# Hybrid decoder trunk on one core: norms applied behind the products, and the modulation vectors spread over VectorE, ScalarE and GpSimd

## The chip, the core and the metric

One core of a Trainium2 chip runs the whole kernel. A core has TensorE (PE, with its weight loads as PEld), VectorE (DVE), ScalarE (ACT), GpSimd (POOL) and SyncE (SP), whose queue issues almost all transfers here. The metric is the device time of one execution in microseconds. The profile gives the span from the first to the last instruction; the time of an execution also holds what lies around the span.

## The reference, cut to what matters

Two layers work on 256 tokens of width 1024. Each layer norms x, scales and shifts it by vectors that come from the conditioning c, multiplies it by a wide matrix, runs three mixers, projects back and adds; then it does the same with an MLP of width 4096. A last norm ends it.

```
for l in range(DEPTH):                                   # 2 layers
    mod = silu_c @ w_ada[l] + b_ada[l]                   # 6 vectors of 1024
    sh1, sc1, g1, sh2, sc2, g2 = jnp.split(mod[:, None, :], 6, axis=-1)
    h = rmsnorm(x, norm1_g[l]) * (1.0 + sc1) + sh1
    proj = h @ w_in[l]
    u, dq, dk, dv, mq, mk, mv = jnp.split(proj, splits, axis=-1)
    ...                                                  # S5, differential attention, MoBA
    x = x + g1 * (mix @ w_out[l])
    h = rmsnorm(x, norm2_g[l]) * (1.0 + sc2) + sh2
    x = x + g2 * (jnp.square(jax.nn.relu(h @ mlp_w1[l])) @ mlp_w2[l])
return rmsnorm(x, final_g)
```

The rsqrt of the norm is one number per token. The shift is one number per channel. With h = x*ag*r + sh, the product is W^T h = r * (W^T (x*ag)) + W^T sh.

## The kernel before

**Layout.** x is kept transposed: channels on the 128 partitions, 256 tokens in the free dimension, eight tiles `xT[0]` to `xT[7]` in one buffer `xall`. Every weight matrix is cut into units of 128x1024 f32 (512 KB). SyncE's queue loads them in program order into a ring `raw` of three. ScalarE rounds a unit to its high half and VectorE subtracts it for the low half, both in `whl`, a ring of four (`unit`, L111 to L125). A product of a unit with a tile `hx` of two halves is three matmuls (`mm3`): high by high, high by low, low by high.

**A norm between products.** After the back projection (`back_unit`, `back_add`) or the last W2 product, `x_ssq` or `square_in` gather squares, `x_norm` (L418) sums them over the channels with matmuls by ones and makes the rsqrt on ScalarE with one Newton step on VectorE. `norm_h` (L453) then calls `h_tile` (L442) eight times: VectorE multiplies x by the gain and the rsqrt into `hz` (L444), ScalarE adds the shift for the high half of `hx` (L449), VectorE takes the low half (L450). Only then can the next product start. This happens in layer 0 ahead of the MLP, in layer 1 ahead of the first product and ahead of the MLP. Layer 0's first norm is written apart and goes tile by tile with the first loads.

**The MLP.** It runs in two halves. A half is eight W1 steps (`mlp1_mm`, two units and 48 matmuls of 256 columns each, both results in one PSUM bank; `mlp1_act` takes relu, square and the two halves) and eight W2 tiles (`mlp2`, two units each). The hidden tiles stay in SBUF.

**The modulation.** Each of the twelve vectors takes eight tiles of 512 KB. The first two of layer 0 are made at the start. Of the rest, five (ADA_DVE) are summed on VectorE, one multiply-add of 128x1024 per tile (L301); two are done by TensorE in steps among the mixer's work; three (ADA_VEC) are loaded ahead as a whole (`ada_load`) and multiplied by TensorE in one go (`ada_vec`, L258) after the norm's sums and before the normed products, one at each of the three norms.

**Order.** Every engine runs its instructions in the order of the program. That order is set by a scheduler which follows priorities; `issue_after` and the letters of MIXER set parts of it by hand. TensorE's `wk` tiles are four PSUM banks, its `acc` tiles another four.

Of the kernel before, what the change touches and what calls it, by code (L numbers as in the profile page):

```python
# [14 lines left out]
OP = mybir.AluOpType  # L15
# [34 lines left out]
UW = 1024  # L50
N_IN, N_OUT, N_W1 = 20, 8, 32
# [4 lines left out]
def hybrid_trunk(ctx, tc, xT_d, pos_d, par_d, sb_d, sbt_d, scw_d, glu_d, wm_d, wa_d, out_d):  # L56
# [55 lines left out]
    def unit(gate=0):  # L112

        w = raw_unit()
        hl = ring.tile([128, 2, UW], F32R, name="whl", bufs=4)
        hi, lo = hl[:, 0, :], hl[:, 1, :]
        if gate:
            with tc.issue_after(gate_a[0].ins):
                V.tensor_copy(hi, w)
            with tc.issue_after((gate_a if gate == 1 else gate_b)[0].ins):  # L120
                V.tensor_tensor(lo, w, hi.bitcast(F32), op=OP.subtract)
        else:
            A.activation(hi, w, AF.Copy)  # L123
            V.tensor_tensor(lo, w, hi.bitcast(F32), op=OP.subtract)  # L124
        return hl  # L125

    last_mm, last_dve, last_act, gate_a, gate_b, gate_t = [None], [None], [None], [None], [None], [None]
# [132 lines left out]

    def ada_load(l, i):

        u = 16 + ADA.index((l, i)) * 8
        ws = []
        for k in range(3):
            w = ring.tile([128, UW], F32, name="ada", bufs=3)
            nc.sync.dma_start(w, wa_d[u + k])
            ws.append([w])
        half = [(n, c) for n, c in (("vv", 2), ("qk", 2), ("sp_gc", 3), ("at_o", 2)) for _ in range(c)]
        half.append(("sp_pb", 1))  # L270
        for k in range(3, 8):
            ws.append([])
            for h in range(2):
                n, c = half.pop(0)
                w = work.tile([128, UW // 2], F32, name=n, bufs=c)
# [1069 lines left out]
```

## Time and profile before

| what | us |
|---|---|
| median of 3 runs (685.09 to 688.39) | 686.48 |
| the profiled execution | 688.0 |
| its span | 686.3 |
| TensorE busy in the span | 664.8 |
| VectorE busy | 510.1 |
| ScalarE busy | 382.8 |
| GpSimd busy | 21.3 |
| mean granted clock of TensorE, share of full speed | 0.993 |

A page of the profile shows one execution. Busy times of an engine are those of its instructions in the records; matmuls are pipelined and their ends are modelled, so a record of 284 ns may stand 120 ns behind the one before it. The chain of waits follows the work that ended last back through what released it. A view by stretches gives the busy time of each engine between two moments.

### The profile page before, as it was taken

What the parts mean: (1) busy time and instruction counts of PE and PEld (TensorE: products, weight loads), DVE (VectorE), ACT (ScalarE), POOL (GpSimd) and SP (SyncE); (2) the same over time, 40 slices, a digit from 0 to 9 for tenths busy, and PEclk for the clock granted to TensorE, in tenths of its full rate; (3) what the DMA queues carried; (4) which work ended last, traced back from release to release, by engine and by line L of the source; (5) the groups of instructions that cost most, each with busy time, mean ns of one, the idle gap of its engine ahead of it and who ended that gap; (6) DMA issues with size and microseconds to landing.
All of it is one profiled execution on the core that took longest, in us unless ns stands there. A gap on an engine that the chain in (4) does not pass through costs nothing. (4 is left out here: it accounts for less than half of the span.)

```text
span 686.3 us, 13334 instructions
## 1 busy us (share of the span) xinstructions
PE 664.8 (97%) x5182; PEld 583.3 (85%) x5182; DVE 510.1 (74%) x1150; ACT 382.8 (56%) x726; POOL 21.3 (3%) x24
## 2 busy tenths in 40 slices
PE   8899999999999999999999999999999999999994
PEld 6686677988899888999887878799899988999884
DVE  7888979986997897879657788886865555555553
ACT  3566744663566833776443556575476533566540
POOL 0000000000000000000210000000000000000221
PEclk9999999999999999999999999999999999999998
DMA  9987776863989688889855532554256555555531
GB/s 323 408 318 241 247 260 241 295 205 113 315 308 334 231 312 264 308 290 338 299 180 192 187 123 89 168 171 158 94 175 194 185 185 188 179 186 184 189 118 61
DMA packets 45134, 151.96 MB, mean 221 GB/s; under 512 B 5136, under 2 KB 5264, under 8 KB 45072
## 3 DMA queue, kind: packets, MB, share of 16 engines
q1 hardware_dynamic: 44640, 150.60, 63.9%
q8 instruction: 40, 0.66, 0.4%
q10 hardware_dynamic: 432, 0.53, 0.2%
q14 instruction: 22, 0.18, 0.1%
HBM read 150.06 MB, written 1.05 MB: 220 GB/s over the span
## 5 line engine op out<-in xcount | busy, mean ns | idle before, releaser
L124 DVE TENSOR_TENSOR whl<-raw,whl 128x1024 fp32r<-128x1024 f32 x178 | 217.1, 1223 | 106.9 <-ACT whl L123 104.4
L123 ACT ACTIVATE whl<-raw 128x1024 fp32r<-128x1024 f32 x178 | 187.9, 1057 | 143.5 <-PE acc L1016 52.5
L132 PE MATMUL wk<-hx,whl 128*128 128x256 f32 x1536 | 188.2, 284 | 1.2 <-DVE hx L450 1.2
L132 PEld LDWEIGHTS wk<-hx,whl 128*128 128x128 f32 x1536 | 185.3, 191 | 4.2 <-DVE hx L450 2.4
L1022 PE MATMUL acc<-mx,whl 128*128 128x512 f32 x240 | 60.7, 395 | 0.0
L132 PE MATMUL acc<-mx,whl 128*128 128x256 f32 x384 | 51.6, 288 | 0.0
L1022 PEld LDWEIGHTS acc<-mx,whl 128*128 128x128 f32 x240 | 43.0, 188 | 8.7 <-issue 0.8
L132 PEld LDWEIGHTS acc<-mx,whl 128*128 128x128 f32 x384 | 47.5, 191 | 3.0 <-issue 2.3
L301 DVE SCALAR_TENSOR_TENSOR adaacc<-ada,cs,adaacc 128x1024 f32<-128x1024 f32 x35 | 44.8, 1280 | 5.8 <-DMA ada<-in_wa_dram 5.7
L1025 DVE SCALAR_TENSOR_TENSOR xall<-acc,mod,xall 128x256 f32<-128x256 f32 x62 | 29.9, 483 | 20.9 <-PE acc L1016 20.2
L132 PE MATMUL acc<-whl,hx 128*128 128x256 f32 x288 | 40.0, 288 | 0.0
L132 PEld LDWEIGHTS acc<-whl,hx 128*128 128x128 f32 x288 | 36.6, 190 | 3.3 <-issue 1.8
L803 PE MATMUL acc<-whl,hx 128*128 128x512 f32 x96 | 38.5, 404 | 0.0
L805 PE MATMUL acc<-whl,hx 128*128 128x512 f32 x96 | 38.4, 400 | 0.0
L804 PE MATMUL acc<-whl,hx 128*128 128x512 f32 x96 | 38.4, 400 | 0.0
L992 ACT ACTIVATE sp_pa<-wk 128x512 f32<-128x512 f32 x32 | 18.9, 592 | 32.7 <-PE wk L132 31.4
L1016 PEld LDWEIGHTS acc<-mx,whl 128*128 128x128 f32 x256 | 34.8, 190 | 2.5
L1016 PE MATMUL acc<-mx,whl 128*128 128x256 f32 x256 | 35.7, 282 | 0.0
L1022 PE MATMUL acc<-at_e,whl 128*128 128x512 f32 x120 | 33.0, 398 | 0.0
L882 ACT ACTIVATE at_e<-at_e,at_m 128x128 f32<-128x128 f32 (+1 forms) x48 | 21.2, 443 | 8.4 <-DVE at_m L877 8.4
L449 ACT ACTIVATE hx<-hz,mod 128x256 fp32r<-128x256 f32 x32 | 14.9, 502 | 19.2 <-DVE hz L444 19.2
L1022 PEld LDWEIGHTS acc<-at_e,whl 128*128 128x128 f32 x120 | 20.7, 191 | 2.7
(381 smaller groups left out, 1005.4 us busy)
## 6 DMA issues: line engine op xcount, KB each, us to landing
raw<-in_wm_dram SPq DMA_DIRECT2D x184, 512.0 KB, 4.0
ada<-in_wa_dram SPq DMA_DIRECT2D x74, 512.0 KB, 5.9
sp_gc<-in_wa_dram SPq DMA_DIRECT2D x9, 256.0 KB, 4.5
qT<-in_wa_dram SPq DMA_DIRECT2D x4, 512.0 KB, 8.9
adaacc<-in_wa_dram SPq DMA_DIRECT2D x3, 512.0 KB, 9.8
qk<-in_wa_dram SPq DMA_DIRECT2D x6, 256.0 KB, 4.9
vv<-in_wa_dram SPq DMA_DIRECT2D x6, 256.0 KB, 4.1
at_o<-in_wa_dram SPq DMA_DIRECT2D x6, 256.0 KB, 4.2
```

The lines of the kernel that those rows point to most:

```text
L123: A.activation(hi, w, AF.Copy)
L124: V.tensor_tensor(lo, w, hi.bitcast(F32), op=OP.subtract)
L132: last_mm[0] = T.matmul(out, a[:, p, :], b[:, q, :], start=start and i == 0, stop=stop and i == 2, skip_group_check=True)
L301: V.scalar_tensor_tensor(acc, w, cs[:, k + j:k + j + 1], acc, op0=OP.mult, op1=OP.add)
L803: T.matmul(o, h[:, 0, sl], w[:, 0, :], start=(k == 0), stop=False, skip_group_check=True)
L804: T.matmul(o, h[:, 0, sl], w[:, 1, :], start=False, stop=False, skip_group_check=True)
L805: last_mm[0] = T.matmul(o, h[:, 1, sl], w[:, 0, :], start=False, stop=last, skip_group_check=True)
L882: A.activation(e[:, c, ks], e[:, c, ks], AF.Exp, scale=SCALE, bias=mx[:, i:i + 1], accum_out=st[:, i:i + 1])
L992: A.activation(r, ps, AF.Relu)
L1016: last_mm[0] = T.matmul(acc[:, :S], w[:, 1, sl], a[:, 0, :], start=False, stop=last, skip_group_check=True)
L1022: T.matmul(acc, w[:, 0, sl], a.rearrange("p c t -> p (c t)"), start=first, stop=False, skip_group_check=True)
L1025: V.scalar_tensor_tensor(xT[f], acc[:, c * S:(c + 1) * S], mvec(l, 5, f), xT[f], op0=OP.mult, op1=OP.add)
```

## The change

Three things are changed together.

First, the tiles that go into three products (layer 1's first product, and W1 in both layers) are x times the gain, not normed (`p_tile`). Each half of such a tile has two columns more, 258 in place of 256, which hold the shift; GpSimd writes them. The product then carries W^T sh in its last columns. On the way out of PSUM, VectorE multiplies the result by `rb`, which holds the rsqrt in 256 columns and ones in the last two (`p_norm`), and ScalarE adds the product's own shift column as a bias, in the relu or in the copy. The two results of a W1 step now take a PSUM bank each. `x_norm` is called inside the first such product, after its second or third k. In layer 1, after the first product (u), the tiles are made once more, normed, for the other products of the mixer.

Second, the gates that put weight units of a norm behind it go (`unit`), and so do the vectors done in one go (`ada_load`, `ada_vec`). VectorE now sums (0,2), (1,0), (1,1), (1,2) and (1,5); for (0,5), (1,3) and (1,4) ScalarE multiplies a tile by its number and GpSimd adds it. Their ends are eight one-column matmuls. `crep` goes, since `cs` is broadcast where it is read.

Third, the steps are placed anew: G in MIXER, GP_STEPS and V_STEPS in the MLP, each issued with a priority that is later by LATE. The ring `ada` has four tiles in place of three, and some buffers are renamed.

```diff
-        if gate:
-            with tc.issue_after(gate_a[0].ins):
-                V.tensor_copy(hi, w)
-            with tc.issue_after((gate_a if gate == 1 else gate_b)[0].ins):
-                V.tensor_tensor(lo, w, hi.bitcast(F32), op=OP.subtract)
...
+    def ada_one(l, i, k, gp):
+        w = ada_tile(l, i, k)
+        if k == 0:
+            ada_st[l, i] = work.tile([128, UW], F32, name="qT", bufs=3) if gp else big.tile([128, UW], F32, name="adaacc")
+        acc, c = ada_st[l, i], cs[:, k:k + 1]
+        if gp:
+            A.activation(w if k else acc, w, AF.Copy, scale=c)
+            if k:
+                GP.tensor_tensor(acc, acc, w, op=OP.add)
+        elif k == 0:
+            V.tensor_scalar(acc, w, c, None, op0=OP.mult)
+        else:
+            V.scalar_tensor_tensor(acc, w, c, acc, op0=OP.mult, op1=OP.add)
+        if k == 7:
+            def fin():
+                cp = wk_tile()
+                for f in range(KT):
+                    T.matmul(cp[:, f:f + 1], acc[:, f * 128:(f + 1) * 128], ones[:, 0:1], start=True, stop=True)
...
+    def p_tile(l, k, ag, i_sh):
+        h = h_buf(k)
+        sh = mvec(l, i_sh, k).to_broadcast([128, SX - S])
+        GP.tensor_copy(h[:, 0, S:], sh)
+        GP.tensor_tensor(h[:, 1, S:], sh, h[:, 0, S:].bitcast(F32), op=OP.subtract)
+        hi, lo = h[:, 0, :S], h[:, 1, :S]
+        A.activation(hi, xT[k], AF.Copy, scale=ag)
+        V.scalar_tensor_tensor(lo, xT[k], ag, hi.bitcast(F32), op0=OP.mult, op1=OP.subtract)
+        return h
+
+    def p_norm(ps):
+        t = work.tile([128, 2, SX], F32, name="sp_pa", bufs=2)
+        for i in range(2):
+            V.tensor_tensor(t[:, i], ps[i][:, :SX], rb, op=OP.mult)
+        return t
...
-            h = norm_h(l, "n1", 0, 1, x_rest(), vec)
-            uT = Chunk("u", h).run().u_out()
-            cm = Chunk("qk", h).run(1)
+            cu = Chunk("p", pts).run(lambda: x_norm(*x_rest()))
+            h = [h_tile(l, k, ag[:, k:k + 1], 0, rb[:, :S]) for k in range(KT)]
+            cm = Chunk("qk", h).run()
+            uT = cu.u_out()
...
-        vec = ada_load(l, 5)
         back_unit(accs, mixed[4:6], False, True)
-        back_add(accs, l, 2)
-        h = norm_h(l, "n2", 3, 4, x_ssq(), vec)
+        ag = norm_gain(l, "n2", 4)
+        pts = []
+        for f in range(KT):
+            back_add(accs, l, 2, f)
+            pts.append(p_tile(l, f, ag[:, f:f + 1], 3))
+        sq = x_ssq()
...
+    GP_STEPS = (1, 1, 1, 1, 2, 2, 2, 2, 1, 1, 1, 1, 2, 2, 0, 0)
+    V_STEPS = (1, 2, 2, 2, 2, 2, 2, 2, 2, 2, 2, 2, 1, 0, 0, 0)
```

How it stands in the engines' order, at three places.

TensorE at layer 1's second norm, before, from the last matmul of the back projection (`mx` are the mixers' results, L387 and L432 the norm's sums, L258 the vector of the modulation done in one go):

```order
L132 MATMUL acc_5684<-mx5_4466,whl_5901 128x256 x3
L387 MATMUL wk_5959<-qT_5957,ones_78 32x256 x4
L387 MATMUL wk_5959<-qT_5958,ones_78 32x256 x2
L432 MATMUL wk_5976<-qT_5958,ones_78 128x256 x2
L432 MATMUL wk_5976<-sq_5972,sel_80 128x256
L258 MATMUL wk_5988<-ada_5865,crep_96 32x256 x4
```

The same place after (L365 and L423 are now the norm's sums, `hx0` the first tile of x by its gain, L127 the product):

```order
L127 MATMUL acc_5747<-mx5_4563,whl_5932 128x256 x3
L365 MATMUL wk_6032<-qT_6030,ones_78 32x256 x4
L127 MATMUL wk_6047<-hx0_5983,whl_6051 128x258 x3
...
L127 MATMUL wk_6047<-hx3_6001,whl_6051 128x258 x2
L365 MATMUL wk_6032<-qT_6031,ones_78 32x256 x2
L127 MATMUL wk_6047<-hx3_6001,whl_6051 128x258
L127 MATMUL wk_6048<-hx3_6001,whl_6056 128x258
L423 MATMUL wk_6077<-qT_6031,ones_78 128x256 x2
L127 MATMUL wk_6048<-hx3_6001,whl_6056 128x258 x2
L127 MATMUL wk_6047<-hx4_6007,whl_6051 128x258
L423 MATMUL wk_6077<-sq_6045,sel_80 128x256
```

The norm's sums moved from ahead of the products into the first step's middle, and the vector of the modulation is gone from there.

TensorE at layer 1's first product, after (L1035 is the last W2 product; L423 the norm's sums; L811 the second product, with the tiles made anew):

```order
L1035 MATMUL acc_4493<-vv_4027,whl_4525 128x256
L127 MATMUL acc_4566<-hx0_4091,whl_4570 128x258 x3
L127 MATMUL acc_4567<-hx0_4091,whl_4570 128x258 x3
L127 MATMUL acc_4566<-hx1_4144,whl_4570 128x258 x3
L127 MATMUL acc_4567<-hx1_4144,whl_4570 128x258 x3
L423 MATMUL wk_4586<-sg_t_4087,ones_78 128x256
L423 MATMUL wk_4586<-sq_4585,ones_78 128x256
L127 MATMUL acc_4566<-hx2_4258,whl_4570 128x258 x3
...
L127 MATMUL acc_4567<-hx7_4553,whl_4610 128x258 x3
L811 MATMUL acc_4673<-whl_4677,hx0_4639 128x512
```

Before, the first product stood behind the norm, and its matmuls alternated with those of the second; now it stands ahead of and around the norm's sums, and the second follows it.

VectorE around layer 0's first W2 half, after (L119 is the low half of a weight unit, L281 and L279 a modulation step, L1044 the addition to x):

```order
L1044 SCALAR_TENSOR_TENSOR xall_74<-acc_2973,mod0_101,xall_74 128x256
L279 TENSOR_SCALAR adaacc_3031<-ada_3029,cs_95 128x1024
L604 SCALAR_TENSOR_TENSOR sg_z_3271<-sg_z_3271,tb_c_2581 128x256
L281 SCALAR_TENSOR_TENSOR adaacc_3031<-ada_3151,cs_95,adaacc_3031 128x1024
L119 TENSOR_TENSOR whl_3122<-raw_3120,whl_3122 128x1024
L119 TENSOR_TENSOR whl_3170<-raw_3168,whl_3170 128x1024
```

GpSimd there, after (the sum of a modulation vector):

```order
L277 TENSOR_TENSOR qT_3020<-qT_3020,ada_3022 128x1024
L277 TENSOR_TENSOR qT_3020<-qT_3020,ada_3143 128x1024
L277 TENSOR_TENSOR qT_3020<-qT_3020,ada_3147 128x1024
L277 TENSOR_TENSOR qT_3020<-qT_3020,ada_3257 128x1024
L277 TENSOR_TENSOR qT_3020<-qT_3020,ada_3261 128x1024
```

GpSimd before, from its set-up on (`sqs` is the sum of squares in the second W2 half):

```order
L96 AFFINE_SELECT mask_82<-mask_82 128x128
L99 IOTA tau_87 128x128
L1039 TENSOR_SCALAR sqs_4022<-sq_4020 128x256
L1041 TENSOR_TENSOR sqs_4022<-sqs_4022,sq_4069 128x256
L1041 TENSOR_TENSOR sqs_4022<-sqs_4022,sq_4163 128x256
```

Before, GpSimd had nothing to do between the set-up and the second W2 half; now it has seven additions in the first W2 half, beside VectorE's own steps.

## Rows read from the trace of the kernel before

The columns stand in the first line of each group. Numbers in brackets at a row's end are idle time ahead of it and what ended it.

**Rows 1.** The first part of the page: busy us, share of the span, instructions.

```profile
PE 664.8 (97%) x5182; PEld 583.3 (85%) x5182; DVE 510.1 (74%) x1150; ACT 382.8 (56%) x726; POOL 21.3 (3%) x24
```

**Rows 2.** Groups of instructions: busy us, mean ns of one, idle time before them.

```profile
L124 DVE TENSOR_TENSOR whl<-raw,whl 128x1024 fp32r<-128x1024 f32 x178 | 217.1, 1223 | 106.9 <-ACT whl L123 104.4
...
L123 ACT ACTIVATE whl<-raw 128x1024 fp32r<-128x1024 f32 x178 | 187.9, 1057 | 143.5 <-PE acc L1016 52.5 <-DMA raw<-in_wm_dram 45.5 <-PE acc L132 13.6
...
L301 DVE SCALAR_TENSOR_TENSOR adaacc<-ada,cs,adaacc 128x1024 f32<-128x1024 f32 x35 | 44.8, 1280 | 5.8 <-DMA ada<-in_wa_dram 5.7
...
L700 DVE TENSOR_TENSOR sp_pa<-wk,tb_c 128x256 f32<-128x256 f32 x16 | 6.7, 416 | 0.8 <-PE wk L696 0.8
...
L444 DVE SCALAR_TENSOR_TENSOR hz<-xall,ag,sp_s 128x256 f32<-128x256 f32 x32 | 14.4, 480 | 0.2
```

**Rows 3.** The chain of waits in order of time: start us, us, what.

```profile
489.50 3.59 PE wk L258 x64
493.09 23.80 PE wk L132 x192
...
517.24 23.13 PE wk L132 x192
540.36 1.84 PE acc L1022 x8
```

**Rows 4.** Busy time of each engine in four stretches of layer 0's MLP.

```profile
core 0: us, PE busy (x) PEld busy (x) DVE busy (x) ACT busy (x) POOL busy (x), PEclk, DMA share, GB/s
173.10:222.30 49.20, 48.02 (x392) 46.94 (x389) 43.23 (x69) 30.77 (x51) 0.00 (x0) 1.00 0.92 319
222.30:269.30 47.00, 47.00 (x280) 40.33 (x279) 39.17 (x60) 26.41 (x45) 0.00 (x0) 1.00 0.77 272
269.30:316.70 47.40, 47.40 (x400) 46.85 (x400) 40.04 (x50) 33.58 (x54) 0.00 (x0) 1.00 0.85 301
316.70:364.20 47.50, 47.50 (x348) 41.92 (x348) 29.71 (x36) 22.20 (x31) 9.44 (x7) 1.00 0.74 253
```

**Rows 5.** Timeline, layer 1's second norm: start us, us, engine, line.

```profile
483.06 0.87 DVE L970 SCALAR_TENSOR_TENSOR xall<-acc,mod,xall 128x256 f32<-128x256 f32 x2
...
486.96 0.88 DVE L970 SCALAR_TENSOR_TENSOR xall<-acc,mod,xall 128x256 f32<-128x256 f32 x2 [0.56 <-PE acc L132]
...
493.02 7.15 PE L132 MATMUL wk<-hx,whl 128*128 128x256 f32 x53
```

**Rows 6.** Timeline of TensorE, layer 1's first norm.

```profile
363.95 0.28 PE L1016 MATMUL acc<-qT,whl 128*128 128x256 f32 x1
...
370.02 0.39 PE L132 MATMUL acc<-hx,whl 128*128 128x256 f32 x1 [0.39 <-ACT hx L449]
...
387.57 0.39 PE L803 MATMUL acc<-whl,hx 128*128 128x512 f32 x1
```

**Rows 7.** Timeline of GpSimd, and of VectorE, at the end of layer 1.

```profile
643.63 1.23 DVE L124 TENSOR_TENSOR whl<-raw,whl 128x1024 fp32r<-128x1024 f32 x1
...
644.14 1.31 POOL L1041 TENSOR_TENSOR sqs<-sqs,sq 128x256 f32<-128x256 f32 x1 [4.18 <-ACT sq L1036]
...
672.23 0.74 POOL L1041 TENSOR_TENSOR sqs<-sqs,sq 128x256 f32<-128x256 f32 x1 [4.31 <-ACT sq L1036]
680.09 1.67 POOL L1232 TENSOR_TENSOR sp_s<-sp_pa,sp_s 128x512 f32<-128x512 f32 x1 [7.12 <-DVE sp_s L439]
```

**Rows 8.** The last multiplies, by their line: duration ns min/median/max, starts.

```profile
L1232 DVE TENSOR_TENSOR qT<-qk,sp_s x2: 692/1220/1748, 680.0 to 680.6; 128x512 f32<-128x512 f32 x2
```

**Rows 9.** Timeline, layer 0's second norm: a weight unit, and TensorE.

```profile
158.31 1.23 DVE L124 TENSOR_TENSOR whl<-raw,whl 128x1024 fp32r<-128x1024 f32 x1 [2.00 <-ACT whl L123]
...
166.92 1.06 PE L387 MATMUL wk<-qT,ones 128*32 128x256 f32 x12
...
182.42 4.82 PE L132 MATMUL wk<-hx,whl 128*128 128x256 f32 x38 [0.35 <-DVE hx L450]
```

More of the change, by code (lines that the diff above doesn't have):

```diff
@@ L228, in ada_finish @@
     def ada_finish(l, i, row):
-        rs = work.tile([128, 256], F32, name="adarow", bufs=1)
+        rs = work.tile([128, 256], F32, name="sg_t", bufs=2)
         A.activation(rs, row, AF.Copy)
@@ L257, in ada_mm @@
             c = (g % per) * 256
-            T.matmul(row[32 * g:32 * g + 32, :], crep[:, k, :], w[g // per][:, c:c + 256],
+            T.matmul(row[32 * g:32 * g + 32, :], cs[:, k:k + 1].to_broadcast([128, 32]), w[g // per][:, c:c + 256],
                      start=(k == 0), stop=(k == 7), tile_position=(0, 32 * g), skip_group_check=True)
[L261 to L275, printed above, removed]
-                nc.sync.dma_start(w, wa_d[u + k, :, h * 512:(h + 1) * 512])
-                ws[-1].append(w)
-        return l, i, ws
@@ L416, in x_ssq, with newton @@
         return (6, 7), p6, sel, qs[6:]
+    rb = const.tile([128, SX], F32)
+    V.memset(rb[:, S:], 1.0)
+    def newton(full, out):
+        y = work.tile([128, S], F32, name="sq", bufs=3)
+        t = work.tile([128, S], F32, name="so_y")
+        with tc.high_priority():
+            A.activation(y, full, AF.Abs_reciprocal_sqrt, scale=1.0 / D)
+            V.scalar_tensor_tensor(t, full, -0.5 / D, y, op0=OP.mult, op1=OP.mult)
+            V.tensor_tensor(t, t, y, op=OP.mult)
+            V.scalar_tensor_tensor(out, t, 1.5, y, op0=OP.add, op1=OP.mult)
     def x_norm(tiles, part, rows, qs):
@@ L805, in add, with run @@
                     last_mm[0] = T.matmul(o, h[:, 1, sl], w[:, 0, :], start=False, stop=last, skip_group_check=True)
-        def run(self, gate=0):
+        def run(self, then=None):
             per = UW // self.n
@@ L810, in run @@
                 if k % per == 0:
-                    w = unit(gate * (1 + k // per) if k < 4 else 0)
+                    w = unit()
                 self.add(k, w[:, :, (k % per) * self.n:(k % per) * self.n + self.n])
+                if then and k == 1:
+                    with tc.issue_after(last_mm[0].ins):
+                        then()
             return self
@@ L1037, in square_in @@
         if f == 0:
-            sqsum[0] = work.tile([128, S], F32, name="sqs", bufs=1)
+            sqsum[0] = work.tile([128, S], F32, name="sg_t", bufs=2)
             GP.tensor_scalar(sqsum[0], q, EPS * D / 128, None, op0=OP.add)
@@ L1201, in hybrid_trunk @@
                         square_in(i - 8)
+                    if half and l + 1 < L:
+                        if i == 8:
+                            ag, nxt = norm_gain(l + 1, "n1", 1), []
+                        nxt.append(p_tile(l + 1, i - 8, ag[:, i - 8:i - 7], 0))
                 j, odd = divmod(slot, 2)
```

239 lines of the change are left out of this document (114 added, 125 removed).

## The prediction

> **What bounds the kernel now.** I read the engine totals first [rows 1]: TensorE is busy 97% of the span and GpSimd 3%. In the groups [rows 2] the largest work of VectorE is the low half of every weight unit (1.22 us each), of ScalarE the high half (1.06 us). The chain of waits [rows 3] runs through TensorE without a gap in both MLP products of layer 1: 192 matmuls of 256 columns in 23.13 us, 120.5 ns each. So a microsecond taken off TensorE there is a microsecond off the time, as long as VectorE, which feeds it, keeps up. How near VectorE is to that shows the table by stage [rows 4]. The four stretches are layer 0's first W1 half, first W2 half, second W1 half and second W2 half. VectorE is busy 43.2 of 49.2, 39.2 of 47.0, 40.0 of 47.4 and 29.7 of 47.5 us: TensorE still sets the pace, with little room. Last I read the three places where a norm stands between products: layer 1's second norm [rows 5], its first norm [rows 6], layer 0's second norm [rows 9]. There TensorE waits for the normed tiles, and one vector of the modulation (3.59 us, 64 records [rows 3]) is put in front of them as filler.
>
> **TensorE's own sum.** The three filler vectors leave TensorE: 3 x 3.59 = 10.8 us, but they stand in the waits, so I book them only with the waits, below. Two more columns cost, by the step from 120.5 ns for 256 columns to 1.84/8 us = 230 ns for 512 [rows 3], 110/256 = 0.43 ns a column, so 0.9 ns a matmul: 768 W1 matmuls a layer and 48 of the first product, 0.7 us in each layer. The modulation's ends (eight one-column matmuls for four wide ones and a transpose) I take as even; eight such ends at up to 0.3 us either way are 2 us in the range.
>
> **Layer 1, second norm.** Before, the last pair of residual additions starts at 486.96, products at 493.02 [rows 5], and four steps of W1 end at 493.09 + 23.80 = 516.9 [rows 3]. After, VectorE has from 483.06 on eight additions and eight low halves (0.87 us for a pair of either) and one square: 4 x 0.87 x 2 + 0.43 = 7.4 us with 0.2 of signals, ending at 490.7. TensorE begins the first step at about 487.3. By the order it meets the norm's matmuls after 20 of the 48 products, so it waits there for the last square: 0.3 us for the signal, 0.6 for two f32 matmuls, about 1.1 for ScalarE, which has a weight unit (1.06) ahead of the partial sums, 0.3 for the last norm matmul: 493.0. The other 28 products take 28 x 0.1214 = 3.4 less the few that slip in between, 2.8: the step ends at 495.8, and three steps of 5.83 at 513.3. Gain 3.6 us; at worst nothing (the wait has only moved), at best 5.
>
> **Layer 1, first norm.** Before, the last W2 matmul is at 363.95, products start at 370.02, and both first products (5.8 and 11.1 us) are through at 387.57 [rows 6]. After, the first product takes tiles that are ready already except the last: it runs from 364.2 for 5.85 us plus 0.65 of norm matmuls, to 370.7. Meanwhile VectorE makes the last tile, three steps of rsqrt (1.3), four scalings (1.75) and the first low half, until about 370.7 too. The second product then needs 48 x 0.231 = 11.1 us, and its tiles come at 0.9 us each plus a weight unit of 1.22 per two tiles, 1.5 against 1.39: 381.9. Gain 5.7 us, at worst 2.
>
> **Layer 0, second norm.** VectorE has two modulation steps (1.28 each) there, which fit into its idle time ahead of the additions (2.00 us ahead of one weight unit alone [rows 9]). With layer 1's 8.9 us from the end of the back projection (166.9) the first step ends at 175.8. GpSimd adds 1.5 (0 to 4.2, below): 177.3, and the second at 183.1. Before, 40 of these 96 products were still to do at 182.42 [rows 9], so 187.2 (40 x 0.12). Gain 4.1.
>
> **VectorE and GpSimd in layer 0's MLP.** Added on VectorE are 32 products from PSUM with the rsqrt; the nearest row is L700 (416 ns, one operand in PSUM [rows 2]), which in succession starts every 0.35 us: 5.6 us for each W1 half. Removed there are six scalings L444 (0.44 each). Modulation steps by the order: 5, 8, 8 and 8 in the four stretches, for 8, 8, 13 and 3 before. Eight new low halves in the last (3.5). So the demand is 43.2+5.6-2.6-3.8 = 42.4; 39.2; 40.0+5.6-6.4 = 39.2; 29.7+6.4+3.5 = 39.6 us [rows 4], against TensorE's 46.6, 46.5, 46.7 and 47.5. Without more, it fits. ScalarE has 24 scalings of 128x1024 more (1.06 each, 25 us) and 32 smaller clamps in place of 16; it is busy 113 of 191 us there [rows 4].
>
> The open price is that of GpSimd's 21 additions of 128x1024, of which 18 fall into this stage. Before it has none; the nearest are a 256-wide one (0.74 us alone; 1.31 when VectorE's low half runs from 643.63, that is until 0.59 after its end) and a 512-wide one of 1.67 us from 680.09 [rows 7]. That last waits for VectorE's first multiply (680.0 plus 0.69), so it takes 1.12 itself, and VectorE's second multiply of the same shape, issued at 680.6, takes 1748 ns against 692 [rows 8]. The two engines shut each other out. From 0.59 at 256 and 1.12 at 512 follows 2.2 us at 1024. Bounds for what one addition costs VectorE: nothing (it falls into idle time) and 2.2; I take 1.9, nearer the 512-wide pair, as VectorE has little idle time left.
>
> The Trainium skill, SBUF — State Buffer, Who interferes with whom, says that a GpSimd instruction reading SBUF holds the shared port for its whole length against VectorE instructions with two SBUF inputs, not against those that read PSUM. The pair above agrees for two SBUF inputs; no run here shows the PSUM side. By the rule an addition would cost nearer 1.7, and the sum would come out some 2 us lower.
>
> Stretch by stretch, with 4, 7, 3 and 4 additions: 42.4+7.6 = 50.0 against 46.6 (carried by the 4 us won at the norm and the weight units that lie ready); 39.2+13.3 = 52.5 against 46.5, 6.0 over; 39.2+5.7 = 44.9, fits; 39.6+7.6 = 47.2 against 47.5, fits barely. So layer 0 wins 4.1 at the norm, loses 6.0 in the first W2 half and 0.7 in columns, and gets back 0.6 from the lead: 2.0 lost. The 16 weight units, 8 tiles of VectorE and 8 of GpSimd in that half are 16.8 MB in 52 us, 320 GB/s; the first stretch ran 319 [rows 4], so DMA bears it.
>
> **Sum.** +2.0 (layer 0) - 5.7 - 3.6 + 0.7 (layer 1's columns) = -6.6 us. The profiled execution took 688.0 (span 686.3 and 1.7 around it), so 681.4 for it; it lay 1.5 above the median of the runs shown, 686.5, which would become 679.9. I say **680.0**.
>
> **Rivals.**
> *GpSimd is hidden.* The additions find VectorE idle or at PSUM work. For it: 39 us of idle VectorE in the four stretches. Against: idle time there lies between waits, and the demand rises. Then the 6.0 vanish and the first W2 half is 0.5 shorter: 673.5. Chance 0.15.
> *The wait has moved.* TensorE stands in order before the norm's matmuls inside the first step. For it: the square comes last on VectorE, the partial sums behind a weight unit on ScalarE. If each of layer 1's norms gives back all but 2 and 0.5 us: -2.5 + 2.0 + 0.7 = +0.2, 686.7; with the additions half hidden 683.5. I put the case at 685, chance 0.22.
> *VectorE saturates: slower.* Place: layer 0's MLP. 18 x 2.1 = 38 us of lock meet 31 us of idle time that is left (191.1 - 152.2, plus what the change adds, 8). The forecast lets nearly all of it be used. If only 15 us can be, 23 us come on top, and with the gains of 4.1, 5.7 and 3.6 and 1.4 for columns that is +11: 697. Slower by 0.5% begins where less than 22 us are used (16 on top). I place the case at 692, chance 0.13.
> *The forecast*, 676 to 683.5: 0.50.
>
> **How the numbers follow.** A change under 0.5%, 3.4 us, can't be told from none, so faster is below 683.1 and slower above 689.9. Faster: hidden 0.15, nearly all of the forecast 0.47: 0.62. Same: the rest of the forecast and most of the moved wait, 0.24. Slower: saturation and a tail of the moved wait, 0.14. The range 672.5 to 688.5 leaves out 2 in 10.
>
> **What would show it.** In the profile after: W1 of layer 1 starting within 1 us of the last residual product, then one wait of 2 to 4 us inside its first step; the first product of layer 1 starting within 0.5 us of the last W2 matmul; W1 steps of layer 1 5.83 us long; GpSimd additions of about 2.2 us, or 3 and more with their wait, and VectorE's low halves of 1.22 us stretched to 2 to 3.4 where they meet; the first W2 half of layer 0 near 52 us, with TensorE waiting for the low halves. Wrong it is if W1 matmuls of 258 columns cost more than 0.122 us, if layer 1's stages are no earlier by 8 to 10 us, or if the W2 half stays at 47 or goes over 58.

## The result, and the profile after

The changed kernel takes 711.97 us (median of 4 runs, 710.38 to 714.04) where the kernel before takes 687.41: ratio 1.0364, 95% interval 1.0320 to 1.0408. It is slower. The prediction, 680.0 us and a range of 672.5 to 688.5, was wrong. The profiled execution took 710.7 us, its span is 709.0 against 686.3.

The first part of the page after, against [rows 1] (busy us, share of the span, instructions):

```profile
PE 668.0 (94%) x5046; PEld 593.2 (84%) x5046; DVE 565.3 (80%) x1202; ACT 423.5 (60%) x789; POOL 96.4 (14%) x93
```

TensorE has 3 us more work but 19.5 us more idle time. VectorE is busy 55 us longer. GpSimd went from 21 to 96 us. The groups of after, against [rows 2] (busy us, mean ns of one, idle time before):

```profile
L119 DVE TENSOR_TENSOR whl<-raw,whl 128x1024 fp32r<-128x1024 f32 x184 | 233.9, 1277 | 64.3 <-ACT whl L118 62.3
...
L277 POOL TENSOR_TENSOR qT<-qT,ada 128x1024 f32<-128x1024 f32 x21 | 59.4, 2831 | 150.8 <-ACT ada L275 136.7
...
L281 DVE SCALAR_TENSOR_TENSOR adaacc<-ada,cs,adaacc 128x1024 f32<-128x1024 f32 x35 | 55.1, 1575 | 5.1 <-DMA ada<-in_wa_dram 5.1
```

The same low half takes 1277 ns on average for 1223 before, the same modulation step 1575 for 1280. That is work of one shape which got longer (35 steps in both; 184 low halves after, 178 in the records of before).

Where the 22.7 us of span come from shows TensorE's timeline, cut at the same events in both kernels:

| stretch | before | after | change |
|---|---|---|---|
| to layer 0's back projection | 129.7 | 129.4 | -0.3 |
| back projection to its end | 37.2 | 43.8 | +6.6 |
| second norm and first W1 half | 55.4 | 52.9 | -2.5 |
| first W2 half | 47.0 | 53.0 | +6.0 |
| second W1 half | 47.4 | 55.0 | +7.6 |
| second W2 half | 47.5 | 59.0 | +11.4 |
| layer 1: first norm and mixer | 122.7 | 119.4 | -3.3 |
| layer 1: second norm and first W1 half | 53.5 | 50.8 | -2.7 |
| layer 1: the rest, and the output | 145.9 | 145.8 | -0.1 |

So each of the three stretches with a changed norm got shorter, 8.5 us together, and layer 0 lost 31.6 elsewhere. The busy times of layer 0, against [rows 4]; the back projection is in the first line, the four stretches of [rows 4] follow:

```profile
core 0: us, PE busy (x) PEld busy (x) DVE busy (x) ACT busy (x) POOL busy (x), PEclk, DMA share, GB/s
129.40:173.22 43.82, 35.55 (x325) 33.32 (x323) 38.08 (x67) 22.09 (x45) 17.66 (x13) 0.92 0.63 218
173.22:226.10 52.88, 52.38 (x420) 49.95 (x419) 51.46 (x80) 40.95 (x69) 11.89 (x4) 1.00 0.77 268
226.10:279.09 52.99, 50.56 (x290) 43.86 (x290) 46.29 (x64) 32.98 (x54) 11.56 (x4) 0.97 0.72 248
279.09:334.07 54.98, 50.10 (x402) 49.68 (x402) 47.18 (x58) 40.58 (x64) 13.96 (x6) 0.97 0.80 281
334.07:393.02 58.95, 53.02 (x371) 47.20 (x369) 49.24 (x57) 29.64 (x42) 19.02 (x25) 0.94 0.72 247
```

Two things are to be seen. VectorE is nearly full only in the stretch of the second norm and the first W1 half (51.5 of 52.9 us), and that stretch got shorter; in the worst stretch it is busy 49.2 of 59.0 us. And the granted clock fell below 1.00 in four of the five, where before it was 1.00 in all.

**What one addition does.** In layer 0's mixer VectorE makes a rsqrt of 128x4 numbers in a chain of operations of some 0.16 us each. Timelines of VectorE, GpSimd and TensorE there (start us, us):

```profile
133.81 0.16 DVE L137 TENSOR_SCALAR rs_i<-at_ms 128x4 int32<-128x4 int32 x1
134.20 2.19 DVE L140 TENSOR_TENSOR rs_t<-rs_i 128x4 f32<-128x4 f32 x1
...
137.42 2.23 DVE L140 TENSOR_TENSOR rs_t<-rs_i 128x4 f32<-128x4 f32 x1
...
139.88 2.19 DVE L142 SCALAR_TENSOR_TENSOR at_rq<-rs_t,rs_i 128x4 f32<-128x4 f32 x1
```

```profile
134.04 2.34 POOL L277 TENSOR_TENSOR qT<-qT,ada 128x1024 f32<-128x1024 f32 x1
...
137.28 4.77 POOL L277 TENSOR_TENSOR qT<-qT,ada 128x1024 f32<-128x1024 f32 x2
```

```profile
134.17 0.39 PE L127 MATMUL acc<-mx,whl 128*128 128x256 f32 x1
142.67 0.66 PE L958 MATMUL wk<-ident,at_on 128*128 128x128 f32 x2 [8.12 <-DVE at_on L953]
```

Three links, 0.16 us of work each, end only when the three additions end, after 2.2 us. TensorE waits 8.12 us for the end of that chain. Behind the wait its clock is down (windows of 2 us, the clock stands behind the busy times):

```profile
142.00:144.00 2.00, 1.33 (x7) 1.36 (x8) 1.97 (x5) 0.00 (x0) 0.05 (x1) 0.50 0.04 8
144.00:146.00 2.00, 2.00 (x12) 2.00 (x11) 1.57 (x5) 0.78 (x2) 0.00 (x0) 0.56 0.32 59
146.00:148.00 2.00, 2.00 (x20) 2.00 (x19) 0.93 (x2) 1.71 (x3) 0.00 (x0) 1.00 0.97 348
```

0.50 is the lower of the two levels, 1.2 GHz: TensorE, back at work from 142.67 on, spends some 3 us at half speed, so some 1.5 us are lost on top of the wait.

**The longest wait in the MLP** is at the first tile of the second W2 half. ScalarE, GpSimd, VectorE, TensorE and SyncE's queue:

```profile
340.45 1.15 ACT L275 ACTIVATE ada<-ada,cs 128x1024 f32<-128x1024 f32 x1 [1.39 <-DMA ada<-in_wa_dram]
341.50 0.40 ACT L1017 ACTIVATE at_on<-sp_pa 128x256 fp32r<-128x256 f32 x1
```

```profile
330.70 2.39 POOL L277 TENSOR_TENSOR qT<-qT,ada 128x1024 f32<-128x1024 f32 x1 [5.92 <-ACT ada L275]
...
341.67 2.34 POOL L277 TENSOR_TENSOR qT<-qT,ada 128x1024 f32<-128x1024 f32 x1 [1.17 <-ACT ada L275]
```

```profile
341.93 2.36 DVE L1018 TENSOR_TENSOR at_on<-sp_pa,at_on 128x256 fp32r<-128x256 f32 x1 [2.95 <-ACT at_on L1017]
```

```profile
344.35 0.80 PE L1041 MATMUL acc<-at_on,whl 128*128 128x512 f32 x1 [5.93 <-DVE at_on L1018]
```

```profile
330.63 3.90 SPq L110 DMA_DIRECT2D raw<-in_wm_dram  x2
334.59 0.91 SPq L255 DMA_DIRECT2D ada<-in_wa_dram  x2
```

TensorE wants one of the last two hidden tiles. Its high half stands on ScalarE behind a scaling (L275), which waits for its tile of weights; the chain of waits puts that tile's load (5.78 us from 334.59) behind GpSimd, which had ended the addition of 330.70 and the first shift columns. But in SyncE's queue the load also stands right behind the loads of two weight units (L110), and the queue is through with these only at 334.53, just after VectorE's low half of 332.20 (1.98 us beside that addition, for 1.22) had ended. Which of the two held the load is not shown. The hidden tile's low half, 0.42 us of work, then meets the next addition and takes 2.36. TensorE waits 5.93 us, and has the lower clock for 6 us more.

### The profile page after: what moved, and what is told of

It reads as the page before. It is cut to its first block, busy times and chain, and to the rows that moved or that the text cites. A ratio compares the mean times of both kernels' runs of the same rounds, so it can differ in the third digit from the quotient of the medians.

```text
span 709.0 us, 13373 instructions
## 1 busy us (share of the span) xinstructions
PE 668.0 (94%) x5046; PEld 593.2 (84%) x5046; DVE 565.3 (80%) x1202; ACT 423.5 (60%) x789; POOL 96.4 (14%) x93
## 4 chain that ended last, share of the span: by engine, by line
PE 53%; DVE 21%; DMA 12%; ACT 7%; issue 6%; POOL 1%; SPq 0%; DVEq 0%; ACTq 0%; POOLq 0%
PE wk L127 13%; PE acc L1041 12%; PE acc L127 8%; PE acc L1035 7%; DMA ada<-in_wa_dram 6%; DVE whl L119 6%; DMA raw<-in_wm_dram 4%; DVE adaacc L281 2%; ACT whl L118 2%; PE wk L886 1%; PE wk L286 1%; PE acc L1038 1%; DMA xall<-in_xT_dram 1%; PE acc L812 1%; PE acc L813 1%
## 5 line engine op out<-in xcount | busy, mean ns | idle before, releaser
L118 ACT ACTIVATE whl<-raw 128x1024 fp32r<-128x1024 f32 x184 | 193.8, 1056 | 161.3 <-PE acc L1035 62.9
L119 DVE TENSOR_TENSOR whl<-raw,whl 128x1024 fp32r<-128x1024 f32 x184 | 233.9, 1277 | 64.3 <-ACT whl L118 62.3
L127 PE MATMUL wk<-hx,whl 128*128 128x258 f32 x1536 | 189.9, 285 | 4.9 <-DVE whl L119 4.9
L127 PEld LDWEIGHTS wk<-hx,whl 128*128 128x128 f32 x1536 | 187.4, 191 | 7.2 <-DVE whl L119 5.3
L277 POOL TENSOR_TENSOR qT<-qT,ada 128x1024 f32<-128x1024 f32 x21 | 59.4, 2831 | 150.8 <-ACT ada L275 136.7
L1041 PE MATMUL acc<-mx,whl 128*128 128x512 f32 x240 | 63.6, 409 | 0.0
L281 DVE SCALAR_TENSOR_TENSOR adaacc<-ada,cs,adaacc 128x1024 f32<-128x1024 f32 x35 | 55.1, 1575 | 5.1 <-DMA ada<-in_wa_dram 5.1
L1041 PEld LDWEIGHTS acc<-mx,whl 128*128 128x128 f32 x240 | 45.0, 197 | 8.5
L127 PE MATMUL acc<-mx,whl 128*128 128x256 f32 x384 | 50.5, 289 | 0.0
L127 PEld LDWEIGHTS acc<-mx,whl 128*128 128x128 f32 x384 | 47.8, 194 | 1.6 <-issue 1.4
L1044 DVE SCALAR_TENSOR_TENSOR xall<-acc,mod,xall 128x256 f32<-128x256 f32 x62 | 29.8, 481 | 19.0 <-PE acc L1035 18.2
L127 PE MATMUL acc<-whl,hx 128*128 128x256 f32 x288 | 39.9, 286 | 0.0
L1011 ACT ACTIVATE sp_pa<-sp_pa 128x256 f32<-128x256 f32 x64 | 31.4, 498 | 14.0 <-DVE sp_pa L465 13.8
L127 PEld LDWEIGHTS acc<-whl,hx 128*128 128x128 f32 x288 | 36.4, 189 | 2.8 <-issue 1.6
L454 POOL CAST hx<-mod 128x2 fp32r<-128x2 f32 x24 | 10.3, 427 | 208.1 <-DVE at_ra L907 120.7
L811 PE MATMUL acc<-whl,hx 128*128 128x512 f32 x96 | 38.5, 406 | 0.0
L1035 PEld LDWEIGHTS acc<-mx,whl 128*128 128x128 f32 x256 | 34.8, 189 | 2.6
L1035 PE MATMUL acc<-mx,whl 128*128 128x256 f32 x256 | 35.6, 281 | 0.0
L465 DVE TENSOR_TENSOR sp_pa<-wk,rb 128x258 f32<-128x258 f32 x64 | 26.5, 419 | 9.2 <-PE wk L127 9.2
```

The source lines that it names most:

```text
L119: (eng or V).tensor_tensor(lo, w, hi.bitcast(F32), op=OP.subtract)
L127: last_mm[0] = T.matmul(out, a[:, p, :], b[:, q, :], start=start and i == 0, stop=stop and i == 2, skip_group_check=True)
L277: GP.tensor_tensor(acc, acc, w, op=OP.add)
L281: V.scalar_tensor_tensor(acc, w, c, acc, op0=OP.mult, op1=OP.add)
L811: T.matmul(o, h[:, 0, sl], w[:, 0, :], start=(k == 0), stop=False, skip_group_check=True)
L1011: A.activation(r[:, i, :S], r[:, i, :S], AF.Relu, bias=r[:, i, S:S + 1])
```

## The experiments

Ratios are to the kernel before, measured beside each run, with a 95% interval; the changed kernel's own is 1.0364. My theory after the profile: GpSimd's additions stop VectorE, and since every queue runs in order, a stop ahead of a link on which TensorE waits becomes a wait of TensorE. Rivals: ScalarE's scalings, a full VectorE, the ends of the vectors, the norm's part itself.

**Without the additions.**

```diff
             A.activation(w if k else acc, w, AF.Copy, scale=c)
-            if k:
-                GP.tensor_tensor(acc, acc, w, op=OP.add)
```

> The changed kernel with GpSimd's 21 additions of 128x1024 left out (ScalarE's scalings, the loads and the ends stay; three modulation vectors are wrong). Theory: each addition shuts VectorE out for its whole 2.4 us, and where a short link of a chain is hit TensorE waits: 8.1 us in layer 0's mixer, 2.0 at the first W2 tile, 2.7 and 2.2 in the second W1 half, 5.9 at the second W2 half. These 21 us go, the stretches at the lower clock behind them too (some 2): 688, 684 to 693. Rival, ScalarE's scalings that wait for their tiles at the head of its queue: they stay, so only the stretched VectorE work comes back and the time stays above 700. Rival, VectorE is full with its own work: above 703.

Measured: 0.9911 (0.9881 to 0.9941), 684.5 us, where I had said 688. The additions alone cost 4.5%, 31 us by the ratios (the two profiled spans differ by 25.7); with sums that cost nothing the change would have been a gain. Low halves are at 1222 ns again. Against the changed kernel the stretches of layer 0 are 8.8 (back projection), 2.1, 4.4, 6.9 and 5.0 us shorter.

**The additions on VectorE.**

```diff
-            A.activation(w if k else acc, w, AF.Copy, scale=c)
-            if k:
-                GP.tensor_tensor(acc, acc, w, op=OP.add)
+            if k:
+                V.scalar_tensor_tensor(acc, w, c, acc, op0=OP.mult, op1=OP.add)
+            else:
+                V.tensor_scalar(acc, w, c, None, op0=OP.mult)
```

> The same vectors, but their 24 steps are multiply-adds on VectorE (1.28 us each, 31 us in all); no addition on GpSimd, no scaling on ScalarE. Theory of the lock: VectorE's busy sum hardly changes (31 us more of steps, about 30 us less of stretched work), but no chain of short operations is stopped any more and ScalarE is free of 25 us: 697, 690 to 703. Rival, VectorE is full: the same work lies on the same engine, 708 to 715.

Measured: 1.0095 (1.0063 to 1.0127), 695.6 us. The same sums on the engine that was said to be short of time are 2.7% faster than on the idle one. The three later stretches of the MLP take 48.2, 48.1 and 50.4 us. What is left is at the mixer's end (50.9 us for 43.8), where steps stand ahead of the same rsqrt chain: a wait of 5.9 us for its result.

**The ends as before.**

```diff
-                for f in range(KT):
-                    T.matmul(cp[:, f:f + 1], acc[:, f * 128:(f + 1) * 128], ones[:, 0:1], start=True, stop=True)
+                for g in range(4):
+                    T.matmul(row[32 * g:32 * g + 32, :], ones, acc[:, g * 256:(g + 1) * 256], start=True, stop=True,
+                             tile_position=(0, 32 * g), skip_group_check=True)
+                return ada_finish(l, i, row)
```

> The changed kernel with the ends of the eight VectorE and GpSimd vectors made as before: four matmuls of 256 columns by ones, a copy, four of 4 columns (0.87 + 0.36 us of TensorE by the trace of before) in place of eight one-column matmuls (1.69 us). If the ends are on TensorE's path: 8 x 0.46 = 3.7 us less, 707 (705 to 709). If they stand in waits that stay: no change, 711.

Measured: 1.0331 (1.0290 to 1.0372), no difference that can be told from 1.0364. It says nothing on the ends: a new wait of 7.9 us for ScalarE's copy between the two parts of an end took what they gave.

**Without the three vectors.**

```diff
     def ada_ones(todo, n):
+        if todo is ada_todo_gp:
+            return
```

> The changed kernel without the three vectors (0,5), (1,3) and (1,4): no loads, scalings, additions, ends (they are set to the bias). It is the price of the norm's part and of the other vectors alone. Theory of the lock: the time of the run without additions less three ends of 1.69 us: 683, 678 to 688. Rival, ScalarE's scalings or the loads cost: lower than the run without additions by 9 us or more. Rival, VectorE is full with its own work or the norm's part itself costs: above 695.

Measured: 0.9762 (0.9727 to 0.9798), 673.7 us. With the three vectors left out, the rest of the change is 2.4% faster. That is a bound and not the norm's own worth, since the kernel before makes these vectors. It is 10.8 us under the run without additions; three ends of 1.69 are 5.1 of them, so scalings and loads cost some 5.7. I had expected 683 and put the border to the rival at 9 us: the scalings and loads do cost, beside the additions; this run can't tell one from the other. Additions (4.5%) and the rest of the three vectors (1.5%), against these 2.4%, make up the 3.6% of the change.

**One input instead of two.**

```diff
-                GP.tensor_tensor(acc, acc, w, op=OP.add)
+                GP.tensor_scalar(acc, w, 1.0, None, op0=OP.mult)
```

> The changed kernel with GpSimd's additions replaced by a multiply of the same 128x1024 with one tensor input (the tile times 1; three vectors are wrong). If any GpSimd instruction of that length shuts VectorE out: each takes some 1.5 to 2.4 us and stretches VectorE's two-input work as before; low halves of up to 3 us, ratio 1.02 to 1.036. If only two-input GpSimd work does: as without additions, 0.99.

Measured: one run, 698.6 us beside 692.2 for the kernel before, whose own runs went from 686.4 to 698.9; so its time tells nothing, its trace does. Some 6 us of it are lost ahead of layer 0's back projection, which starts at 135.64 for 129.44: behind a wait of 1.88 us for a load, TensorE is at the lower clock for 17.1 us there. GpSimd is no shorter at it (2.78 us in the median, for 2.41), and VectorE hardly notices. The line of the low halves (duration ns, least, median, most), first here, then in the changed kernel:

```profile
L119 DVE TENSOR_TENSOR whl<-raw,whl x184: 1204/1225/1873, 18.0 to 676.6; 128x1024 fp32r<-128x1024 f32 x184
```

```profile
L119 DVE TENSOR_TENSOR whl<-raw,whl x184: 1196/1224/3159, 17.9 to 688.8; 128x1024 fp32r<-128x1024 f32 x184
```

GpSimd's instruction of 2.77 us now holds a low half up by 0.65 us at most; of the 25 low halves that ran beside one, 20 were not stretched. One operation of the 128x4 chain still took 1.04 us. The second W1 half takes 48.1 us, as without additions, so its 6.9 us came from the stops of VectorE. The second W2 half still takes 57.0, with a wait of 4.3 us at the same hidden tile. Its chain of waits (start us, us):

```profile
320.34 2.77 POOL qT L277
323.11 0.04 POOL hx L454
323.15 6.14 DMA ada<-in_wa_dram
...
329.37 0.16 ACT ada L275
329.53 0.90 issue
330.43 0.41 ACT at_on L1017
```

That is a second way in which the three vectors cost time: the load comes late, and the scaling that waits for it holds up ScalarE's queue. The chain puts the late load on GpSimd, which is done with the tile at 323.11; but SyncE's queue was busy with a weight unit's load until 323.10 itself. Whether GpSimd's end alone made the load late is not shown.

**Quarters.**

```diff
-                GP.tensor_tensor(acc, acc, w, op=OP.add)
+                for q in range(0, UW, 256):
+                    GP.tensor_tensor(acc[:, q:q + 256], acc[:, q:q + 256], w[:, q:q + 256], op=OP.add)
```

> The changed kernel with every GpSimd addition cut into four of 128x256. If VectorE waits for the instruction at hand alone, its short operations wait 0.6 us at most in place of 2.4: the rsqrt chain in layer 0's mixer loses 2 to 3 us instead of 6.1 and the other waits shrink; ratio 1.02 (1.01 to 1.028). If the whole of GpSimd's work counts, since the next quarter takes over at once: 1.034 to 1.04.

Measured: 1.0202 (1.0113 to 1.0290). The chain in the mixer, VectorE's timeline:

```profile
132.89 0.66 DVE L138 TENSOR_SCALAR rs_i<-rs_i 128x4 int32<-128x4 int32 x1
133.59 0.65 DVE L140 TENSOR_TENSOR rs_t<-rs_i 128x4 f32<-128x4 f32 x1
...
135.23 0.65 DVE L140 TENSOR_TENSOR rs_t<-rs_i 128x4 f32<-128x4 f32 x1
135.91 0.65 DVE L141 SCALAR_TENSOR_TENSOR rs_t<-at_ms,rs_t 128x4 f32<-128x4 f32 x1
```

A link ends after 0.65 in place of 2.2 us; TensorE's wait there is 3.9 for 8.1. VectorE waits for the instruction at hand, and gets its turn between two. That shortens the back projection (40.5 us for 43.8) and the second W1 half (49.6 for 55.0), but not the two W2 halves (54.2 and 58.6 for 53.0 and 59.0). In the second of these a wait of 5.7 us stands at the same hidden tile as in the changed kernel. That half took 57.0 us with one input, 54.0 without additions and 49.2 without the three vectors, so a good part of the 11.4 us lost there is not VectorE's stops.

**The additions in the MLP alone, and the same steps on VectorE.** In both kernels (0,5) is made on TensorE in the mixer, nothing stands at the mixer's end, and 16 steps lie in the three later stretches.

```diff
-    ADA_PE = ((0, 3), (0, 4))
+    ADA_PE = ((0, 3), (0, 4), (0, 5))
...
-    GP_STEPS = (1, 1, 1, 1, 2, 2, 2, 2, 1, 1, 1, 1, 2, 2, 0, 0)
+    GP_STEPS = (0, 0, 0, 0, 1, 1, 1, 1, 1, 1, 1, 1, 2, 2, 2, 2)
```

On VectorE:

> The run with VectorE's multiply-adds, but (0,5) made on TensorE in the mixer like (0,3) and (0,4), none of the steps at the mixer's end, and the 16 steps of (1,3), (1,4) in the three later stretches of layer 0's MLP. Theory: the wait of 5.9 us at the mixer's end and the low clock behind it go (8), TensorE gets 3.59 more and an end of 1.69 less: 695.6 - 6 = 689.5, ratio 1.000 (0.994 to 1.005). Rival, VectorE is full in the MLP (each stretch at 45 to 47 us of work against 46.6): waits for low halves come back there, 1.01.

> The same kernel as the run with (0,5) on TensorE and (1,3), (1,4) on VectorE, once more beside the next ones: ratio 0.9925 as before (0.989 to 0.996).

On GpSimd:

> The kernel with (0,5) on TensorE, but the 16 steps of (1,3) and (1,4), at the same places in the last three stretches of layer 0's MLP, are ScalarE scalings and 14 GpSimd additions in place of VectorE's multiply-adds; none stands in the mixer. Theory: in the MLP too an addition costs TensorE about 1 us (the changed kernel's last three stretches were 4.4, 6.9 and 5.0 us longer than without additions, with 12 of them): some 12 us over the VectorE steps, ratio 1.01 (1.002 to 1.02). Rival: only the short chain in the mixer is hurt, and VectorE's idle time hides the rest: 0.990 to 0.996.

Measured: VectorE 0.9925 (0.9886 to 0.9964), and 0.9949 (0.9904 to 0.9994) beside the GpSimd form, which has 1.0164 (1.0103 to 1.0226). Sixteen scalings and fourteen additions cost 2.1% more than sixteen multiply-adds, 15 us, a little over 1 us for each addition on average, with no short chain of the mixer near them. It is no price for each: the first and second stretch after the first W1 half take 51.9 and 59.2 us for 46.9 and 49.7, with seven of the additions by the trace; the first W1 half with two of them (48.9 in both) and the second W2 half with five (48.2 for 48.7) lose nothing. In the second stretch 10.2 us at the lower clock are part of the loss. The VectorE form is faster than both kernels; I had expected 1.000 of it.

**The same with ends as before.**

To the edit of the ends above comes a flush at two more places:

```diff
-W11 O F1 Km K0 P1 P12 Ks
+W11 O G0 F1 Km G0 K0 P1 P12 Ks
```

> That kernel with the ends of the seven VectorE vectors made of four matmuls of 256 columns, a copy and four of 4 columns, the two halves of an end kept apart by one step of the plan (two more places for them in layer 0's mixer). If an end costs 1.69 against 1.23 us on TensorE's path: 7 x 0.46 = 3.2 us less, ratio to before 0.988. If the copy on ScalarE makes TensorE wait again, as in the earlier run with such ends: 0.992 or above.

Measured: 0.9927 (0.9886 to 0.9968). It can't be told from 0.9949. Its wait for ScalarE's copy is 1.7 us.

**The norms in layer 1 alone.** From the kernel before: layer 0 keeps its normed tiles and (0,5) as filler; (1,4) and (1,5) go to VectorE's plan.

```diff
-    ADA_VEC = ((0, 5), (1, 4), (1, 5))
-    ADA_DVE = ((0, 2), (1, 0), (1, 1), (1, 2), (1, 3))
+    ADA_VEC = ((0, 5),)
+    ADA_DVE = ((0, 2), (1, 0), (1, 1), (1, 2), (1, 3), (1, 4), (1, 5))
...
-            h = norm_h(l, "n1", 0, 1, x_rest(), vec)
-            uT = Chunk("u", h).run().u_out()
-            cm = Chunk("qk", h).run(1)
+            cu = Chunk("p", pts).run(lambda: x_norm(*x_rest(), out=rb_new()))
+            h = [h_tile(l, k, ag[:, k:k + 1], 0, rbs[0][:, :S]) for k in range(KT)]
+            cm = Chunk("qk", h).run()
+            uT = cu.u_out()
```

> The kernel before with the norms behind the products in layer 1 alone (the first product and W1); layer 0 keeps its normed tiles and the one filler vector (0,5). (1,4) and (1,5), the other two fillers, become VectorE steps, in layer 0's last W2 half and layer 1's first W1 steps, where VectorE is idle for 18 and 18 us; ends as before. No addition of a vector on GpSimd. Theory: layer 1's two norms give back what the changed kernel showed, 5.4 and 3.9 us (its stage was 2.7 shorter with an end of 1.7 in it where before had 0.5), less 0.9 for each of two ends: -7.5 us, ratio to before 0.989 (0.985 to 0.994). Rival, VectorE's 16 more steps or the products from PSUM cost it again: 0.997 to 1.01.

> The norms behind the products in layer 1 alone, once more: the Newton steps have priority as in the changed kernel, and the buffers of layer 0 are those of before (TensorE's order up to the first W2 half is that of before). The earlier run lost 8.7 us ahead of layer 0's back projection and 3.5 at layer 1's first norm. Theory: both losses were made by buffers and priorities, not by the norm's part: ratio 0.989 (0.985 to 0.994). Rival: VectorE's steps for (1,4) and (1,5) cost it: 0.997 or above.

Measured: 1.0001 (0.9962 to 1.0040) and 0.9975 (0.9941 to 1.0010). No gain that can be told, against 0.989 expected, twice; putting priorities and buffers back did not bring it. What both profiled runs lost ahead of layer 0's back projection (8.7 and 6.8 us) goes in the main with the clock: TensorE spent 13.7 and 17.1 us at the lower level there, after waits of 1.8 to 3.6 us for loads of the modulation. In the second run (its profiled execution took 694.3 us, the median is 689.0) layer 1's first norm and mixer took 124.4 us, none less than before (122.7), with a wait of 2.6 us for the second product's tiles and 3.4 us at the lower clock behind it; its second norm gave 1.9. Its trace shows why the tiles were late: two modulation steps of 1.27 us stand on VectorE ahead of the norm's last square, and on ScalarE the rsqrt stands behind a weight unit that waits 3.06 us for its load. In the changed kernel no step stood there. So the rival, the steps of (1,4) and (1,5), has part of it; no run leaves only these two steps out.

## Why the prediction was wrong, point by point

**TensorE's columns.** Mis-sized, at no loss. A W1 half of layer 1 with 258 columns takes 46.19 us for 384 matmuls, 120.3 ns each, where 256 took 120.5 [rows 3]:

```profile
561.53 1.68 PE wk L286 x16
...
607.95 46.19 PE wk L127 x384
```

Two more columns cost nothing; I had booked 1.4 us.

**The ends.** The first of these two lines is one end, 1.68 us. I had taken it as even with the old one, 0.3 at most either way. In the timeline of before an end is 0.56 for the wide matmuls (not 0.87, as I still wrote for the run with such ends) and 0.34 for the small ones. Five such and three of 0.34 make 5.5 us, eight of 1.68 make 13.4: 7.9 us of TensorE's own time were left out. It had to be asked how a one-column matmul is paid. Eight of them leave sixteen records, 0.11 us apart, hardly less than the 0.120 of a matmul with 258 columns, and each record has a load of 128x128 weights of its own (192 ns in the records). That the load sets this pace is inferred from these rows; no run shows it apart.

**Layer 1's second norm.** Right in place, and nearly in size. TensorE after, against [rows 5]:

```profile
512.33 0.76 PE L365 MATMUL wk<-qT,ones 128*32 128x256 f32 x8
513.01 2.67 PE L127 MATMUL wk<-hx,whl 128*128 128x258 f32 x20
515.62 0.63 PE L365 MATMUL wk<-qT,ones 128*32 128x256 f32 x4
...
517.99 7.22 PE L127 MATMUL wk<-hx,whl 128*128 128x258 f32 x57
```

W1 starts 0.7 us behind the residual products, as forecast, and the wait of 2 to 4 us that I expected inside the first step is not there at all. From the end of the back projection to W2 the gain is 2.7 us with an end of 1.68 where before had 0.34, so 4.0 for the norm (forecast 3.6). The rival in which the wait only moves is out for this place.

**Layer 1's first norm.** Right at the place. After, against [rows 6]:

```profile
393.02 1.59 PE L127 MATMUL acc<-hx,whl 128*128 128x258 f32 x12
394.45 0.59 PE L423 MATMUL wk<-sg_t,ones 128*128 128x256 f32 x2
394.88 0.59 PE L423 MATMUL wk<-sq,ones 128*128 128x256 f32 x2
395.12 4.70 PE L127 MATMUL acc<-hx,whl 128*128 128x258 f32 x36
399.66 0.40 PE L811 MATMUL acc<-whl,hx 128*128 128x512 f32 x1
```

The first product runs through without a wait and the second follows; 48 matmuls at 0.23 bring them to 410.8, 17.8 us from the last W2 product, where I had 17.7. But to the end of the mixer only 3.3 of the 5.7 us are left: what follows the products did not come earlier by as much. At the first matmul of the S5's output (L723 at 400.99 before, L729 at 426.17 after) the gain is already down to 3.6. I had stopped counting at the products.

**Layer 0's second norm.** Forecast 4.1 with 1.5 for GpSimd; measured 2.5 to the end of the W1 half, with one end (1.8 us) in it. Without additions it is 4.6. Right in place, and near in size.

**VectorE and GpSimd: the step that failed.** The price of one addition was about right: 2.34 to 2.40 us alone for an estimate of 2.2 from [rows 7] and [rows 8]. What failed is how the prices were put together, at four points.

First, I priced 18 of the 21 additions, those in the MLP, with four, seven, three and four in its stretches; that the first W2 half has seven, as the text on the change says too, is wrong. By the trace there are four, four, five and two, and six stand ahead of layer 0's second norm, where I put none on the path. Three of those met the rsqrt chain, and the back projection lost 6.6 us.

Second, I compared VectorE's sum in a stretch with TensorE's: 44.9 and 47.2 against 46.7 and 47.5 "fit". The stretches took 55.0 and 59.0, with VectorE at 47.2 and 49.2 us, its idle time unused. An in-order queue doesn't spread a stop over idle time. GpSimd, VectorE, ScalarE and TensorE in the second W1 half:

```profile
308.56 5.92 POOL L277 TENSOR_TENSOR qT<-qT,ada 128x1024 f32<-128x1024 f32 x2 [16.63 <-ACT ada L275]
```

```profile
309.14 3.09 DVE L119 TENSOR_TENSOR whl<-raw,whl 128x1024 fp32r<-128x1024 f32 x1
312.16 3.41 DVE L281 SCALAR_TENSOR_TENSOR adaacc<-ada,cs,adaacc 128x1024 f32<-128x1024 f32 x1
```

```profile
315.94 0.51 ACT L1011 ACTIVATE sp_pa<-sp_pa 128x256 f32<-128x256 f32 x1 [3.04 <-DVE sp_pa L465]
```

```profile
318.29 15.95 PE L127 MATMUL wk<-hx,whl 128*128 128x258 f32 x118 [2.22 <-DVE whl L119]
```

A low half and a step of VectorE took 3.09 and 3.41 us beside two additions, ScalarE's relu waited 3.04 for the product from PSUM behind them, the high half of a weight unit stood behind that relu, and TensorE waited 2.22. Its other wait there, 2.67, came from a step of VectorE that stood 1.84 us for its tile's load. The first W2 half came out at 53.0 for 52.5, right by accident, with four additions where I had counted seven: its tiles from 249.49 on run at TensorE's pace of 5.58 us; the surplus is waits of 2.4 us at its first tile (for hidden tiles, not for low halves), the low clock behind them, and ends.

Third, ScalarE's 24 scalings were counted as 25 us that fit beside 113 of 191. A scaling also waits for its load, at the head of a queue on which hidden tiles hang; the run without the vectors puts 5.7 us on scalings and loads together.

Fourth, the clock. I had TensorE at full clock throughout, and priced a wait at its own length. In layer 0 the granted clock was 0.92, 0.97, 0.97 and 0.94 in four stretches, at the lower level for 3 to 6 us behind four of the five longest waits (8.1, 5.9, 2.2 and 2.0 us; not behind the one of 2.7).

**The rivals.** "VectorE saturates: slower" named the right place and sign, at 0.13, but not the mechanism: in the stretches that lost, VectorE does not fill up. It put 16 to 23 us on top; the additions cost 26 to 31, through order, and the run on VectorE itself is faster. "GpSimd is hidden" and "the wait has moved" are out. The Trainium skill, SBUF — State Buffer, Who interferes with whom, says that a VectorE instruction with at most one SBUF input, outside the two-port modes, does not contend with GpSimd, and that one with two does, against a GpSimd instruction that reads SBUF. The trace of the changed kernel agrees: 64 products from PSUM (L465) took 407 to 428 ns, not one of them stretched, six of them beside an addition, while operations on two SBUF inputs waited up to the whole addition. For a GpSimd instruction with one input the second half of it goes too far: there GpSimd's 2.77 us held a low half up by 0.65 at most, and 20 of 25 not at all.

## What to carry to other kernels

Work that is handed to an idle engine is not free if that engine shuts out a busy one: ask for each of its instructions which short operation on a chain it can meet, and price it at its full length there, not against idle time in the sum of a stretch. All 24 steps on the busy engine itself, 1.28 us each, made the loss of 3.6% one of 1.0%. With one vector given back to TensorE and the other 16 steps placed in the MLP, away from the chains, the change gained 0.5 to 0.8%; the same 16 on the idle engine lost 1.6%. And a wait of TensorE can cost more than its length: expect the lower clock behind it, and look it up in the trace.

## What was not expected of the hardware

- An operation of VectorE on 128x4 elements, 0.16 us of work, took 2.19 to 2.23 us behind a GpSimd addition of 128x1024, and 0.65 behind one of 128x256.
- A GpSimd instruction of the same shape with one tensor input (2.77 us alone) held VectorE up by 0.65 us at most on its low halves; one took 6.1 us in the mixer, beside four VectorE operations of 1.2 to 1.3 us.
- A f32 matmul of 258 columns (f32r) cost 120.3 ns, no more than one of 256; an end of eight one-column f32 matmuls cost 1.68 us, nearly twice that of four with 256 columns and four with 4.
- TensorE's clock was at the lower level for 3 to 6 us after four of the five waits of 2 to 8 us, and the full level came back while it worked at the lower one. In two other runs (the one with one input, and the second with the norms in layer 1 alone) 17.1 us at the lower level followed a wait of 1.9 us.
